# Multi-query attention: value scaling on GpSimd moved beside the VectorE exponential, a later first VectorE exponential, and a new plan

## The chip, the cores and the metric

The kernel runs on one core of one Trainium2 chip. The metric is device time in microseconds (us) of that core, from launch to the end of the program; lower is better. Before the change the median of three runs is 757.11 us (756.61 to 757.47). The profiled execution took 757.08 us, of which 755.2 us lie between its first and last instruction (the span), so a time is about 1.9 us more than its span.

## What is computed

The reference is attention with 16 query heads and one shared head of keys and values, for 8 batches, 1024 positions and a head dimension of 64, all in fp32:

```python
scores = q @ k.T / sqrt(64)
weights = exp(scores - max) / sum(exp(scores - max))
out = weights @ v
```

There are 8 x 16 x 1024 x 1024 = 134 million exponentials. The kernel does not subtract the maximum, and it gets the sum of the weights from a column of ones beside the values.

## The kernel before

Two heads are handled as a pair. There are 64 pairs (8 per batch), and each pair has 8 tiles of 128 keys. So there are 512 tiles, and each tile is scored in two halves of 512 queries: 1024 scores in all, each 128 keys by 2 heads by 512 queries. A score (`score`, L482) is two matmuls on TensorE that fill one of three PSUM buffers, `sc0` to `sc2`; I call them slots. A slot is free again when the exponential has read it.

The exponentials are split between two engines.

- Most are ACTIVATE instructions on ScalarE (ACT in the profile; `exp_act`, L496, recorded at L498), one per score, which write fp16 weights into a ring of 23 buffers `w`. Before the change there are 804 of them.
- The other 110 tiles (220 scores) are done by VectorE (DVE; `exp_dve`, L504). VectorE first reads each score from PSUM, scales it and writes a 16-bit integer, the `z` instruction (L512). When both halves are there, three or four more instructions on 128x2048 elements in SBUF build three terms `z`, `m` and `e` whose sum, with three scaled copies of the values, is the exponential's product: two masks (L529 and L532), a square of `m` (L524) and a product of `z` and `m` (L536). In the plan they are steps 0, 1, 2 and 3. Before the change step 2 squares only 1216 of the 2048 columns on VectorE, and GpSimd (POOL) squares the other 832 in two pieces of 416 (`sq`). Step 4 is the alternative: VectorE squares all 2048 columns. The plan takes it where more than `QUEUE` pieces are still waiting for GpSimd (L274).

The weights, which are laid out with keys on partitions, are the stationary operand of the value products (`value`, L555): 128x65 matmuls that accumulate into one of two PSUM buffers, for three groups of 6, 4 and 6 query blocks per pair (`BLOCKS`). A tile of ScalarE needs one value product per query block, a tile of VectorE three. In the plan an `av` is two such matmuls. After a group's last product VectorE takes the reciprocal of the sums (`rec`, L578) and multiplies (`norm`, L587), and the pair's output leaves by DMA.

Each batch needs its values three times, scaled by the three `TERMS` (`val`, L378). The first batch's are scaled on VectorE; the other seven batches' 21 scalings run on GpSimd. Both the pieces and these scalings are started by the helper `beside` of the kernel (L540): it adds a wait, so that the GpSimd instruction starts when the VectorE instruction before the chosen one has ended. So it runs beside the chosen one.

The order of the work on every engine is fixed when the program is built. `plan` (L56) walks through the work with a cost for each instruction, and the order in which it lets things happen is the order in which the instructions are recorded; on the chip an engine keeps that order and waits on semaphores. The planner's choices that matter here are these.

- Which tiles VectorE takes (L120 to L128): a tile is taken if the work waiting for VectorE is below `BACKLOG`, or `BACK_END` when at most `END` pairs are left, and none of the last `LAST` tiles is taken.
- When TensorE scores rather than multiplies values (L176 to L189, `MARGIN` and `WAIT`), and how far the value products lag behind the scores (L170, `LAG`, `RAMP`, `END_LAG`).
- `SPLIT`: for the last `SPLIT` tiles all first halves are scored before all second halves.
- What runs on GpSimd beside what: the planner's own `beside` (L71) takes the oldest waiting piece of work that has waited for an age. It is called for squares beside a `z` (L245), for values beside a `rec` (L256), and for both wherever they have waited longer than `PIECE_AGE` (L230).

At the start TensorE transposes keys and queries, VectorE copies them out of PSUM, and the second half of this is recorded between the first scores (`turn_first`, L442).

Of the kernel before, what the change touches and what calls it, by code (L numbers as in the profile page):

```python
# [20 lines left out]

ACT_P, ACT_L = 0.905, 1.19
QK_P, AV_B, AV_1, SWITCH, PE_L = 0.22, 0.0295, 0.02, 0.10, 0.49
MARGIN, WAIT = 0.318, 0.144
END, END_LAG = 5.567, -0.028
VEC = dict(z=1.13, rec=0.11, val=0.34)
NORM = 0.07, 0.067
STEPS = (0.6, 0.6, 0.7, 1.13)
WHOLE, QUEUE = 1.13, 3
PIECE, PIECE_T, PIECE_AGE = 416, 1.2, 11.627  # L30
VEC_L = 0.19
VEC_DEP = 0.12
BACKLOG, BACK_END = 8.576, 2.062
LAST, SPLIT, FIRST = 13, 7, 3
RAMP, VALS, COLD, WARM = 0.541, 3.0, 1, 0.0
BUSY = 20, 3, 5, 0
WBUFS = 23
ZBUFS = 6
LAG = 2.1
FAR = 1e9  # L40
BLOCKS = (0, 6, 10, 16)
STEP = 2
# [13 lines left out]
def plan(NP, NKT, HP=8):  # L56
# [6 lines left out]
    def vec(k, g):  # L63
        return NORM[0] + NORM[1] * size[g] if k == "norm" else VEC[k]
# [3 lines left out]
    def emit(t, *op):  # L68
        ops.append((t, len(ops), op))

    def beside(t, age, kinds):  # L71

        x = next((x for x in pool if x[0] <= t - age and x[1] in kinds), None)
        if x is None:
            return
        pool.remove(x)
        emit(t, *x[1:])
        if x[1] == "val":
            vdone[x[2:]] = t + PIECE_T
        elif x[3] == 1:  # L80
            squared.append((t + PIECE_T, x[2]))

    squared: list = []
    pe = act = dve = 0.0
    mode = ""
    slot = [0.0] * 3
    acc = [0.0] * 2
# [18 lines left out]
    while p < NP or groups:  # L106
        assert min(pe, dve) < 2e3
        if pe <= dve:
            T = pe
# [40 lines left out]
            for grp in groups:  # L150
# [7 lines left out]
                for j, k, x in left:  # L158
                    t = NKT * gp + j
# [9 lines left out]
            rest = (2 * NT - nq) / (2 * NKT)  # L169
            lag = min(LAG, END_LAG + (LAG - END_LAG) * rest / END, RAMP * nq / (2 * NKT))  # L170
            cost = AV_B * STEP * cold
# [18 lines left out]
            if do == "qk":  # L190
                s = min(free, key=lambda s: slot[s])
                st = max(T + (SWITCH if mode != "qk" else 0), slot[s])
                pe, mode = st + QK_P * cold, "qk"
# [6 lines left out]
                else:  # L200
                    u = units.pop(0)
                    act = max(act, st + PE_L + QK_P * (cold - 1))
# [5 lines left out]
            elif do == "av":  # L208
                st = max(T + (SWITCH if mode != "av" else 0), tav)
                pe, mode = st + cost + (AV_1 if mode == "qk" else 0), "av"  # L210
                grp, (j, k, x) = pick
                gp, gg, left, a, n, known = grp
                t = NKT * gp + j
# [11 lines left out]
            else:  # L225
                nxt = [x for x in slot + acc + [tav] if T < x < FAR] + [dve] * (dve > T)
                pe = max(min(nxt, default=0.0), T + 1e-3)
        else:
            T = dve
            beside(T, PIECE_AGE, ("sq", "val"))  # L230
            steps += [(x[1], len(STEPS) - 1) for x in squared if x[0] <= T]
            squared = [x for x in squared if x[0] > T]
# [6 lines left out]
            what, x = (free or todo or [("", None)])[0]  # L239
            if z:  # L240
                x = z[0]
                zs.remove(x)
                r, s, u = x
                T = max(T, r)
                beside(T, 0.3, ("sq",))  # L245
                emit(T, "z", *u)
                dve = T + VEC["z"]
                slot[s] = dve + VEC_L
                if u[1] == 1:
                    steps += [(u[0], n) for n in range(len(STEPS) - 1)]  # L250
                    ready[u[0], 1, "v"] = dve + VEC_L
                last = ("z", u[0])
            elif what == "ev":
                evs.remove(x)
                if x[1] == "rec":
                    beside(T, 0.3, ("val",))  # L256
                emit(T + late, *x[1:])
                dve = T + late + vec(x[1], x[3])
                if x[1] == "rec":
                    evs.insert(0, (T, "norm", *x[2:]))  # L260
                else:
                    acc[x[4]] = dve + VEC_L
                last = x
            elif what == "val":
                vals.remove(x)
                emit(T, "val", *x[1:])
                dve = T + VEC["val"]
                vdone[x[1:]] = dve + VEC_L
                last = None
            elif what == "step":  # L270
                steps.remove(x)
                dve = T + late + STEPS[x[1]]
                if x[1] == len(STEPS) - 2:
                    if sum(y[1] == "sq" for y in pool) > QUEUE:  # L274
                        x, dve = (x[0], len(STEPS)), T + late + WHOLE
                        steps.append((x[0], len(STEPS) - 1))
                    else:
                        pool += [(dve, "sq", x[0], n) for n in range(2)]
                emit(T + late, "step", *x)
                if x[1] in (0, len(STEPS) - 1):  # L280
                    ready[x[0], x[1] and len(TERMS) - 1, "v"] = dve + VEC_L
                last = x
            else:
                nxt = [x[0] for x in zs + evs + vals + squared if x[0] > T] + [pe + 1e-6] * (pe > T)
                dve = max(min(nxt, default=0.0), T + 1e-3)
                last = None
# [7 lines left out]
def kernel(  # L294
# [37 lines left out]

    wbuf = [consts.tile([P, 2, S], FP16, name=f"w{i}") for i in range(WBUFS)]
    order, vtiles = plan(NP, NKT, HP)

    writers: dict = {}
# [100 lines left out]
    def busy(n):  # L437

        for _ in range(n):
            nc.tensor.matmul(kst[0]["busy"][:, 0, 0:P], ident, ident, start=True, stop=True)  # L440

    def turn_first(n):  # L442
# [5 lines left out]
        if n == 0:  # L448
# [7 lines left out]
            for r in range(2):  # L456
                V(out=k16[:, 0:4, r, :], in_=kn[:, 0:4, :])
            busy(BUSY[0])
        parts = ((0, 2), (2, 4)) if n == 0 else ((4, NKT),)
# [6 lines left out]
        if n == 0:  # L466
            busy(BUSY[1])
        if n < 2:
# [7 lines left out]
        if n == 0:  # L476
            V(out=qn[0][:, 4:NKT, :], in_=qf[:, 4:NKT, :])
            for r in range(2):
                V(out=k16[:, 4:NKT, r, :], in_=kn[:, 4:NKT, :])
            busy(BUSY[2])  # L480

# [146 lines left out]
    with tc.manual_schedule(engines={ENG.PE, ENG.Activation, ENG.DVE, ENG.Pool}):  # L628
# [7 lines left out]
        for _, _, (op, *args) in order:  # L636
            if op == "qk":
# [7 lines left out]
                if scores < 3:  # L645
                    busy(BUSY[3])
                if scores == 3:
# [46 lines left out]
```

## Time and profile before

| | before |
|---|---|
| time, median of 3 runs | 757.11 us |
| span of the profiled execution | 755.2 us |
| TensorE matmul busy | 737.0 us (98%) |
| TensorE weight load busy | 493.1 us (65%) |
| VectorE busy | 710.3 us (94%) |
| ScalarE busy | 739.5 us (98%) |
| GpSimd busy | 335.3 us (44%) |
| ScalarE exponentials, first start and last end | 804, 6.57 us and 746.13 us |
| one `z` of VectorE (128x1024 from PSUM) | 1.21 us |
| one square of 1216 columns; product of 2048 columns | 0.78 us; 1.22 us |
| one piece of 416 columns on GpSimd | 0.87 us |
| one value scaling on GpSimd | 1.48 to 2.02 us |

Three engines look nearly full. To read which one sets the time, two things about the view are needed. An instruction's duration runs from its start to its end; on ScalarE an instruction can start before the one ahead of it has ended, so that durations overlap, and the pace is the distance between two starts or two ends, not the duration. And a matmul's end is modelled, so a busy TensorE need not be at its limit.

### The profile page before, as it was taken

What the parts mean: (1) busy time and instruction counts of PE and PEld (TensorE: products, weight loads), DVE (VectorE), ACT (ScalarE), POOL (GpSimd) and SP (SyncE); (2) the same over time, 40 slices, a digit from 0 to 9 for tenths busy, and PEclk for the clock granted to TensorE, in tenths of its full rate; (3) what the DMA queues carried; (4) which work ended last, traced back from release to release, by engine and by line L of the source; (5) the groups of instructions that cost most, each with busy time, mean ns of one, the idle gap of its engine ahead of it and who ended that gap; (6) DMA issues with size and microseconds to landing.
All of it is one profiled execution on the core that took longest, in us unless ns stands there. A gap on an engine that the chain in (4) does not pass through costs nothing.

```text
span 755.2 us, 30412 instructions
## 1 busy us (share of the span) xinstructions
PE 737.0 (98%) x13804; PEld 493.1 (65%) x13804; DVE 710.3 (94%) x1057; ACT 739.5 (98%) x806; POOL 335.3 (44%) x398
## 2 busy tenths in 40 slices
PE   7899999999999999999999999999999999999997
PEld 4455666666666666666666666666666666666676
DVE  6999999999999999999999999999999999999963
ACT  7999999999999999999999999999999999999995
POOL 2357434473444643446344564345533555343210
PEclk9999999999999999999999999999999999999999
DMA  6564555647556457675446756457644466644133
GB/s 129 89 99 103 89 103 89 107 89 111 114 107 107 95 86 105 121 111 102 92 74 122 135 88 101 76 98 134 121 87 88 77 127 115 104 78 100 34 86 86
DMA packets 179889, 75.10 MB, mean 99 GB/s; under 512 B 78384, under 2 KB 178736, under 8 KB 179760
## 3 DMA queue, kind: packets, MB, share of 16 engines
q1 hardware_dynamic: 140544, 54.01, 32.8%
q0 software_dynamic: 37744, 18.36, 21.5%
q8 instruction: 108, 1.77, 1.0%
q10 hardware_dynamic: 1472, 0.79, 0.4%
q14 instruction: 21, 0.17, 0.1%
HBM read 39.58 MB, written 33.55 MB: 97 GB/s over the span
## 4 chain that ended last, share of the span: by engine, by line
ACT 91%; PE 6%; DVE 2%; DMA 0%; issue 0%; DVEq 0%
ACT w_109 L498 4%; ACT w_112 L498 4%; ACT w_113 L498 4%; ACT w_111 L498 4%; ACT w_110 L498 4%; ACT w_114 L498 4%; ACT w_108 L498 4%; ACT w_102 L498 4%; ACT w_107 L498 4%; ACT w_98 L498 4%; ACT w_97 L498 4%; ACT w_106 L498 4%; ACT w_104 L498 4%; ACT w_96 L498 4%; ACT w_115 L498 4%; ACT w_100 L498 4%
## 5 line engine op out<-in xcount | busy, mean ns | idle before, releaser
L486 PEld LDWEIGHTS <-k2t_135 64*128 64x128 f16 x256 | 13.3, 94 | 20.2 <-issue 12.5
L486 PEld LDWEIGHTS <-k2t_1158 64*128 64x128 f16 x256 | 12.2, 93 | 10.7 <-issue 4.3
L486 PEld LDWEIGHTS <-k2t_14686 64*128 64x128 f16 x256 | 12.4, 93 | 9.2 <-issue 1.8
L486 PEld LDWEIGHTS <-k2t_7903 64*128 64x128 f16 x256 | 12.4, 93 | 8.2 <-issue 1.8
L486 PEld LDWEIGHTS <-k2t_5642 64*128 64x128 f16 x256 | 12.3, 93 | 8.2 <-issue 1.8
L486 PEld LDWEIGHTS <-k2t_12425 64*128 64x128 f16 x256 | 12.3, 93 | 8.2 <-issue 1.8
L486 PEld LDWEIGHTS <-k2t_10164 64*128 64x128 f16 x256 | 12.3, 93 | 8.2 <-issue 1.8
L486 PEld LDWEIGHTS <-k2t_3381 64*128 64x128 f16 x256 | 12.0, 93 | 7.8 <-issue 1.6
L565 PEld LDWEIGHTS <-w_100 128*128 128x128 f16 x288 | 12.9, 97 | 4.7 <-issue 4.7
L565 PEld LDWEIGHTS <-w_102 128*128 128x128 f16 x288 | 12.8, 97 | 4.5 <-issue 4.5
L565 PEld LDWEIGHTS <-w_104 128*128 128x128 f16 x288 | 12.9, 97 | 4.2 <-issue 4.2
L565 PEld LDWEIGHTS <-w_96 128*128 128x128 f16 x288 | 12.9, 98 | 4.1 <-issue 4.1
L565 PEld LDWEIGHTS <-w_106 128*128 128x128 f16 x288 | 13.0, 97 | 3.6 <-issue 3.6
L565 PEld LDWEIGHTS <-w_98 128*128 128x128 f16 x288 | 12.9, 97 | 3.7 <-issue 3.7
L565 PEld LDWEIGHTS <-w_115 128*128 128x128 f16 x272 | 12.2, 97 | 4.2 <-issue 4.2
L565 PEld LDWEIGHTS <-w_101 128*128 128x128 f16 x288 | 12.7, 97 | 3.3 <-issue 3.3
L565 PEld LDWEIGHTS <-w_105 128*128 128x128 f16 x288 | 12.7, 97 | 3.3 <-issue 3.3
L565 PEld LDWEIGHTS <-w_103 128*128 128x128 f16 x288 | 12.6, 97 | 3.4 <-issue 3.4
L565 PEld LDWEIGHTS <-w_97 128*128 128x128 f16 x288 | 12.7, 97 | 2.9 <-issue 2.7
L565 PEld LDWEIGHTS <-w_108 128*128 128x128 f16 x272 | 12.2, 97 | 3.5 <-issue 3.5
L565 PEld LDWEIGHTS <-w_113 128*128 128x128 f16 x272 | 12.2, 97 | 3.6 <-issue 3.6
L565 PEld LDWEIGHTS <-w_117 128*128 128x128 f16 x272 | 12.0, 97 | 3.8 <-issue 3.8
(5615 smaller groups left out, 3712.2 us busy)
## 6 DMA issues: line engine op xcount, KB each, us to landing
qf<-in_q_dram ACTq DMA_DIRECT2D x2, 256.0 KB, 3.8
qn_185<-in_q_dram POOLq DMA_DIRECT2D x1, 512.0 KB, 6.4
qn_328<-in_q_dram POOLq DMA_DIRECT2D x4, 128.0 KB, 3.9
qn_504<-in_q_dram POOLq DMA_DIRECT2D x4, 128.0 KB, 3.5
out_dram<-osb_501 SPq DMA_DIRECT2D x1, 512.0 KB, 3.2
out_dram<-osb_821 SPq DMA_DIRECT2D x1, 512.0 KB, 5.3
qn_1011<-in_q_dram POOLq DMA_DIRECT2D x4, 128.0 KB, 3.2
out_dram<-osb_1149 SPq DMA_DIRECT2D x1, 512.0 KB, 3.2
```

The source lines that it names most:

```text
L486: nc.tensor.matmul(sc[t, c][:, h, :], kst[p // HP]["k2t"][64 * h : 64 * h + 64, key(p // HP, j, h), :], qt[p][64 * h : 64 * h + 64, 4 * c ...
L498: ins = nc.scalar.activation(out=w, in_=sc.pop((t, c)), func=EXP, scale=ascale).ins
L565: nc.tensor.matmul(acc[p, grp][:, o : o + D + 1], w[:, h, i * P : (i + 1) * P], kst[p // HP]["v"][k][:, j, 0 : D + 1], start=(n == 0 and y ...
```

## The change

The diff does four things.

1. Values are scaled on GpSimd beside a `z` (which reads PSUM) and no longer beside a reciprocal. A scaling must have waited three times as long as a square before it is taken.
2. The planner's VectorE is taken to be ready only at 2.0 (`READY`), so that three scores go to ScalarE before the first one goes to VectorE; before, the first VectorE score was the second of all.
3. `QUEUE` falls from 3 to 1, so that step 4 (the whole square on VectorE) is chosen at times.
4. The planner's other constants get new values, and with all of this the order on every engine is a new one.

Counted from the order in which the two programs record their work:

| | before | after |
|---|---|---|
| ScalarE exponentials | 804 | 808 |
| tiles on VectorE (`z` instructions) | 110 (220) | 108 (216) |
| squares in pieces: VectorE parts, GpSimd pieces | 110, 220 | 82, 164 |
| whole squares on VectorE (step 4) | 0 | 26 |
| `av` (two value matmuls each) | 5856 | 5824 |
| runs of scores between value products | 650 | 616 |
| `av` after the last score | 112 | 115 |

```diff
-MARGIN, WAIT = 0.318, 0.144
-END, END_LAG = 5.567, -0.028
+MARGIN, WAIT = 0.284, 0.166
+END, END_LAG = 1.121, -0.195
...
-WHOLE, QUEUE = 1.13, 3
-PIECE, PIECE_T, PIECE_AGE = 416, 1.2, 11.627
+WHOLE, QUEUE = 1.13, 1
+PIECE, PIECE_T, PIECE_AGE = 416, 1.2, 10.459
...
-BACKLOG, BACK_END = 8.576, 2.062
-LAST, SPLIT, FIRST = 13, 7, 3
-RAMP, VALS, COLD, WARM = 0.541, 3.0, 1, 0.0
-BUSY = 20, 3, 5, 0
+BACKLOG, BACK_END = 7.719, 2.337
+LAST, SPLIT, FIRST = 12, 2, 3
+RAMP, VALS, COLD, WARM = 0.162, 3.0, 1, 0.0
+BUSY, READY = (20, 3, 5, 0), 2.0
...
-LAG = 2.1
+LAG = 1.753
...
-        x = next((x for x in pool if x[0] <= t - age and x[1] in kinds), None)
+        x = next(
+            (x for x in pool if x[0] <= t - age * (1 + 2 * (x[1] == "val"))
+             and x[1] in kinds), None)
...
-    pe = act = dve = 0.0
+    pe, act, dve = 0.0, 0.0, READY
...
-                beside(T, 0.3, ("sq",))
+                beside(T, 0.3, ("sq", "val"))
...
-                if x[1] == "rec":
-                    beside(T, 0.3, ("val",))
```

## The prediction

> **What bounds the kernel now.** I read the page first: its busy line and the chain that ended last.
>
> ```profile
> PE 737.0 (98%) x13804; PEld 493.1 (65%) x13804; DVE 710.3 (94%) x1057; ACT 739.5 (98%) x806; POOL 335.3 (44%) x398
> ...
> ACT 91%; PE 6%; DVE 2%; DMA 0%; issue 0%; DVEq 0%
> ```
>
> Three engines are above 90%, so busy shares alone do not decide. The chain says ScalarE (91%). To be sure, I read its pace in the timeline, start and duration of its last exponentials:
>
> ```profile
> 723.70 1.35 ACT L498 ACTIVATE w_118<-sc_0_17375 128x1024 f16<-128x1024 f32 x1
> 724.62 1.35 ACT L498 ACTIVATE w_118<-sc_1_17379 128x1024 f16<-128x1024 f32 x1
> ...
> 743.67 1.55 ACT L498 ACTIVATE w_105<-sc_1_17927 128x1024 f16<-128x1024 f32 x1
> 744.57 1.56 ACT L498 ACTIVATE w_106<-sc_1_17930 128x1024 f16<-128x1024 f32 x1
> ```
>
> The starts are 20.87 us apart over 23 exponentials, 0.907 each, but the durations grow, so starts run ahead of the work. The ends (start plus duration) go from 725.05 to 746.13: 0.9166 each. The ends give the true pace. The first three exponentials of the run show the same: starts 6.57, 7.49, 8.40 with durations 1.02, 1.02, 1.03 end at 7.59, 8.51, 9.43. Over the run the first ends at 6.57 + 1.02 = 7.60 and the last at 746.13: 738.5 us for 803 intervals. At 0.9167 they are 736.1. So ScalarE lost only 2.4 us between its first and last exponential. The waits name where:
>
> ```profile
> ACT w_108 L498 <- PE sc_0_1407 L486: 0.9, 1, 0.9
> ACT w_96 L498 <- PE sc_1_212 L486: 0.4, 1, 0.4
> ACT w_99 L498 <- PE sc_1_282 L486: 0.3, 1, 0.3
> ACT w_109 L498 <- PE sc_0_531 L486: 0.2, 1, 0.2
> ```
>
> Taken between ends rather than from idle time, the losses are 0.48 at 9.4 us (w_96), 0.40 at 13.6 (w_99), 0.29 at 31.4 (w_109), 0.24 at 70.2 (w_107), 1.01 at 72.3 (w_108) and 0.05 at 19.5: 2.46 in all. After 72.3 us no interval between ends is longer than 0.92. ScalarE is the bound without a gap for 674 us, and nothing that only makes TensorE or VectorE shorter can be seen in the time there.
>
> What caused these waits is in TensorE's waits, and in the timeline around 70 us:
>
> ```profile
> PE sc_1_212 L486 <- DVE z_206 L512: 1.3, 1, 1.3
> PE sc_0_1351 L486 <- DVE z_1317 L512: 0.8, 1, 0.8
> PE acc_0_1265 L565 <- DVE m_886 L536: 0.6, 1, 0.6
> PE sc_0_237 L486 <- DVE z_206 L512: 0.5, 1, 0.5
> ```
>
> ```profile
> 67.39 1.35 DVE L524 TENSOR_TENSOR m_1205<-m_1205 128x1216 f16<-128x1216 f16 x1
> ...
> 68.07 2.02 POOL L378 TENSOR_SCALAR vals_1_88<-vn_907 128x512 f16<-128x512 f32 x1
> ...
> 70.26 1.76 DVE L536 TENSOR_TENSOR m_886<-z_834,m_886 128x2048 f16<-128x2048 f16 x1
> ...
> 72.11 1.49 POOL L378 TENSOR_SCALAR vals_2_89<-vn_907 128x512 f16<-128x512 f32 x1 [1.18 <-DVE m_886 L536]
> ```
>
> The two early losses come from the very first VectorE exponential, z_206: VectorE is still copying queries, so z_206 holds a slot from the second score on until 9.31. The pair at 70.2 and 72.3 is the first batch of GpSimd scalings: a square of 1216 columns took 1.35 (0.78 elsewhere), a product 1.76 (1.22 elsewhere), beside GpSimd work; the late `z` and the late `m_886` stop TensorE.
>
> **What the Trainium skill says.** "Perfetto Trace Analysis", section "Identifying the Most-Contended Engine": for ScalarE and VectorE occupancy is a fair measure, for matmuls it is not, and weight-load share should be used. That fits: TensorE's 98% stands beside 65% weight load, and ScalarE's 98% is the one to believe. "SBUF — State Buffer", section "Who interferes with whom": a VectorE instruction with at most one SBUF input outside the two-port modes does not contend with GpSimd; one with two SBUF inputs contends with GpSimd's reads. "VectorE: DVE Perf Modes", section "Why PSUM operands drop a tier": with a PSUM operand the two-port mode is out. So a `z` is a good neighbour. The trace agrees: vals_2_89, beside a reciprocal and a `z` only, took 1.49; vals_1_88, which began beside a square, took 2.02, and that square 1.35. "TensorE: Matmul & The Clock Gate", section "What's actually happening": a quiet TensorE drops to half clock in windows of 3413 ns. The trace shows 0.50 granted at 28 to 31 us, after value products had nearly stopped from 22 to 26 us (0.2 us busy); the loss at 31.4 lies in it.
>
> **The change, part by part.**
>
> *Four more ScalarE exponentials* (804 to 808, counted from the order): 4 x 0.917 = +3.67 us. They lie on the bound; nothing hides them.
>
> *First VectorE exponential behind three scores.* Now scores 1 to 3 go to ScalarE, score 4 is the `z`, in the slot that the first exponential leaves at about 7.6; VectorE reaches it at about 8.2, as now (the copy ahead of it, 0.42 from 7.76, is unchanged), and gives it back at about 9.4. The fourth ScalarE score uses the slot freed at 8.5 (second exponential's end) and is there by 9.0 (0.39 for the matmuls), while ScalarE needs it at 9.4. The next one takes z's slot at 9.4 and is needed at 10.3. So both early losses go: -0.48 - 0.40 = -0.88. The first exponential still starts at 6.57: nothing ahead of it changes.
>
> *Values beside `z`.* 21 GpSimd scalings move; their time falls from 1.5 to 2.0 each to about 1.5, off the path. On the path are only the losses at 70 us, 1.25. Bounds: none or all of it goes. The order around it is new and the collision was with squares too, so I take three quarters: -0.94. The scaling now waits for the VectorE instruction ahead of a `z`; queued behind it on GpSimd are pieces of squares, for which products (L536) wait, and the DMA issues for queries. With 44% of GpSimd in use, less after, there is room for that. In later batches the same scalings cost ScalarE nothing (no long interval after 72.3).
>
> *VectorE.* Two tiles fewer: 2 x (2 x 1.21 + 0.68 + 0.68 + 0.78 + 1.22) = -11.6. 26 whole squares at 1.22 (the nearest row is the product of 2048 columns) for 0.78: +11.4. Net nothing: still some 710 busy, 94%, and 26 products that no longer wait for pieces, with GpSimd relieved of 56 x 0.87 = 49 us. TensorE has 64 value matmuls fewer, at 0.030 (six start 0.18 apart in the tail) -1.9. Both are hidden behind ScalarE.
>
> *Half clock at 31 us.* The new order leaves TensorE as quiet as the old one: 13 `av` between the 20th and the 34th score now, 10 in the new order. I keep the 0.29, so the difference is 0.
>
> *End.* The last score still takes a slot that was freed three exponentials before the last, and then TensorE has 115 `av` instead of 112 without idle time: 6 x 0.030 = +0.18. The output after it is the same.
>
> *New waits.* An irregular order could bring some: bounds 0 and 1.5 (as the whole of the losses at 70 us and a bit more). VectorE's slack is what guards against it; I take +0.2.
>
> Sum: 757.11 + 3.67 + 0.18 - 0.88 - 0.94 + 0.2 = 759.34, so 759.3 us.
>
> **Rivals.**
>
> *All losses go, none come:* 757.11 + 3.67 + 0.18 - 2.46 = 758.5, within 0.2% of before (up to 758.62). For it: the losses are few and the change aims at four of six. Against: the clock loss has no reason to go. This is the floor if ScalarE's pace stands. Chance 0.13.
>
> *VectorE becomes late:* whole squares put 26 x 0.44 us back in bursts; a late `z` holds a slot and stops TensorE, as z_1317 did for 0.8. With 2 us of such waits: 759.3 + 2 = 761.3. For it: VectorE is 97% busy between 150 and 550 us. Against: it is so now, and loses nothing. Chance 0.15.
>
> *The other side, faster:* ScalarE's pace would be TensorE's in truth, with scores just in time and 0.9035 between starts as ScalarE's own. Then time follows TensorE: -1.9 and -1.8 for the early losses, 753.4. For it: 44% of the exponentials start within 0.05 us of their score's modelled end. Against: ends spaced 0.917 even where starts are 0.903 apart, at the beginning and at the end. Chance 0.04.
>
> **Numbers.** My forecast has 0.68, and all of it is slower by over 0.2%. Slower 0.68 + 0.15 = 0.83; same 0.13; faster 0.04. The range goes from 758.0 (the floor 758.5, less the 0.5 by which single runs differ from the median) to 761.4 (the late VectorE).
>
> **What would show it.** Right: 808 exponentials ending 0.917 apart with under 2 us lost in all; no loss at 9.4 and 13.6; GpSimd scalings at 1.5; about 9.1 us from the last exponential's end to the end of the span, plus 0.2. Wrong: ends closer than 0.915, or long intervals after 100 us, or a first exponential that does not start at 6.57.

## The result, and the profile after

The changed kernel takes 761.39 us, the median of four runs (760.57 to 764.25), beside 757.26 for the kernel before on the same chip. By the medians it is slower by 4.1 us. The ratio, taken over all runs, is 1.0063 (95% interval 1.0036 to 1.009), which is 4.8 us. The forecast was 2.2. The profiled execution took 760.57, with a span of 758.8. First its page, busy line and chain that ended last:

```profile
PE 730.6 (96%) x13740; PEld 487.8 (64%) x13740; DVE 712.4 (94%) x1045; ACT 743.9 (98%) x810; POOL 286.4 (38%) x342
...
ACT 79%; PE 11%; DVE 6%; POOL 2%; issue 1%; POOLq 0%
```

GpSimd's busy time fell by the forecast 49 us, VectorE's is the same within 2, TensorE's is 6 lower, and ScalarE has four exponentials more. The busy shares explain nothing beyond those four. The chain does tell something: ScalarE has fallen from 91% to 79% of it, and GpSimd, which was not in it, has 2%. This points to waits of ScalarE behind work that ends on GpSimd, though chain shares alone don't show it. ScalarE's own waits (in all, times, longest) name the place:

```profile
ACT w_96 L498 <- PE sc_1_3910 L486: 1.3, 1, 1.3
...
ACT w_104 L498 <- PE sc_0_1184 L486: 0.2, 1, 0.2
ACT w_115 L498 <- PE sc_1_14985 L486: 0.2, 1, 0.2
```

I use one measure throughout: the ends of exponentials are 0.9167 apart, and what an interval between two ends is longer than that is a loss. A loss is placed at the end that comes late, but for those of 9.4 and 13.6 us, which keep the prediction's names (it placed them at the end before). With the losses, the span divides almost without a rest. The second column of measurements is a second profile of the same changed kernel (`e0_after_again` below); all are differences from the profile before, in us.

| term | predicted | after, span 758.8 | after again, span 760.3 |
|---|---|---|---|
| four more exponentials | +3.67 | +3.67 | +3.67 |
| start of the first one (6.57 before; 6.03, 6.37) | 0 | -0.55 | -0.20 |
| losses up to 80 us (2.47 before; 0.43, 1.55) | -1.82 | -2.04 | -0.92 |
| losses after 80 us (0 before; 2.69, 2.70) | +0.20 | +2.69 | +2.70 |
| last end to end of span (9.08 before; 8.90, 8.88) | +0.18 | -0.18 | -0.20 |
| sum | +2.23 | +3.59 | +5.05 |
| measured span less 755.2 | | +3.6 | +5.1 |

One term stands out: the losses after 80 us, the same in both executions, and thirteen times the 0.2 that I took for "new waits". The largest is 1.46 at 178 us, at w_96. I followed it back. TensorE's waits say that its score waited for a slot that a `z` held:

```profile
PE sc_1_3910 L486 <- DVE z_3743 L512: 1.9, 1, 1.9
```

The timeline of VectorE there (start, duration, line, operation, output and inputs; in brackets the idle time before it and what ended it):

```profile
168.60 1.22 DVE L512 TENSOR_SCALAR z_3743<-sc_0_3731 128x1024 uint16<-128x1024 f32 x1
...
169.83 1.06 DVE L532 TENSOR_SCALAR m_3695<-z_3607 128x2048 uint16<-128x2048 uint16 x1
...
171.14 2.06 DVE L524 TENSOR_TENSOR m_3695<-m_3695 128x1216 f16<-128x1216 f16 x1
173.96 1.23 DVE L536 TENSOR_TENSOR m_3278<-z_3173,m_3278 128x2048 f16<-128x2048 f16 x1 [0.77 <-POOL m_3278 L524]
...
175.80 1.21 DVE L512 TENSOR_SCALAR z_3743<-sc_1_3868 128x1024 uint16<-128x1024 f32 x1
```

And that of GpSimd:

```profile
166.56 1.49 POOL L378 TENSOR_SCALAR vals_1_85<-vn_3070 128x512 f16<-128x512 f32 x1 [1.93 <-DVE osb_3681 L587]
168.00 0.78 POOL L403 DMA_DIRECT2D qn_3692<-in_q_dram  x1
168.86 1.48 POOL L378 TENSOR_SCALAR vals_2_86<-vn_3070 128x512 f16<-128x512 f32 x1
170.30 0.75 POOL L403 DMA_DIRECT2D qn_3692<-in_q_dram  x1
171.07 0.89 POOL L524 TENSOR_TENSOR m_3278<-m_3278 128x416 f16<-128x416 f16 x1
171.90 0.76 POOL L403 DMA_DIRECT2D qn_3692<-in_q_dram  x1
172.68 1.24 POOL L524 TENSOR_TENSOR m_3278<-m_3278 128x416 f16<-128x416 f16 x1
```

Read together: both scalings take their 1.48 us beside a `z`, as intended. But the places beside a `z` are where the squares' pieces went before. The two pieces of tile 98 (m_3278) lose their places, grow older than `PIECE_AGE`, and the planner then starts them beside whatever VectorE does next. On the chip they start later still: GpSimd works almost without a pause from 166.56 until 174.64, on two scalings, two pieces and four DMA issues of 0.75 to 0.78 (`beside` in the kernel records a waiting issue behind each piece of work). So the first piece, recorded beside a reciprocal, starts 1.3 us after it and runs beside another tile's square of 1216 columns, which takes 2.06 instead of 0.78; the second, beside the same square, takes 1.24 instead of 0.87. The product of m_3278 must then wait 0.77 for GpSimd, and behind it in VectorE's order, after a reciprocal and a multiplication, stands the second half of z_3743, which starts at 175.80 although its score has been there since 173.6. Its slot stops TensorE for 1.9, and ScalarE for 1.3. The Trainium skill says in "SBUF — State Buffer", section "Who interferes with whom", that VectorE with two SBUF inputs contends with GpSimd's reads. The trace agrees: the square overlaps the two pieces by 0.82 and 0.52, together 1.34, and grew by 1.28.

Counted from the two orders, the pieces up to 700 us that do not run beside a `z` are 2 before (one of tile 28 at 67 us, one of tile 87 at 153) and 11 after, from tiles 35, 98, 183, 290, 327, 355 and 415. The losses at 178, 297, 504, 547 to 554 and 636 us follow such pieces within some 14 us. Those at 64 and 622 us (0.29 and 0.11) follow none, and behind the late pieces of tiles 35 and 290 (77 and 446 us) nothing is lost.

Three predicted details hold. No loss is left at 9.4 and 13.6, and the scalings take 1.48 to 1.50, all 21. The pace at the end is the old one; the last exponentials of the changed kernel end at 747.15, 748.06, 748.98 and 749.90:

```profile
745.63 1.52 ACT L498 ACTIVATE w_107<-sc_0_17738 128x1024 f16<-128x1024 f32 x1
746.55 1.51 ACT L498 ACTIVATE w_108<-sc_0_17743 128x1024 f16<-128x1024 f32 x1
747.45 1.53 ACT L498 ACTIVATE w_107<-sc_1_17786 128x1024 f16<-128x1024 f32 x1
748.36 1.54 ACT L498 ACTIVATE w_108<-sc_1_17789 128x1024 f16<-128x1024 f32 x1
```

### The profile page after: what moved, and what is told of

It reads as the page before. It is cut to its first block, busy times and chain, and to the rows that moved or that the text cites. A ratio compares the mean times of both kernels' runs of the same rounds, so it can differ in the third digit from the quotient of the medians.

```text
span 758.8 us, 30190 instructions
## 1 busy us (share of the span) xinstructions
PE 730.6 (96%) x13740; PEld 487.8 (64%) x13740; DVE 712.4 (94%) x1045; ACT 743.9 (98%) x810; POOL 286.4 (38%) x342
## 4 chain that ended last, share of the span: by engine, by line
ACT 79%; PE 11%; DVE 6%; POOL 2%; issue 1%; POOLq 0%
ACT w_97 L498 4%; ACT w_101 L498 4%; ACT w_98 L498 4%; ACT w_99 L498 4%; ACT w_100 L498 4%; ACT w_96 L498 4%; ACT w_102 L498 4%; ACT w_103 L498 4%; ACT w_104 L498 3%; ACT w_116 L498 3%; ACT w_108 L498 3%; ACT w_106 L498 3%; ACT w_118 L498 3%; ACT w_107 L498 3%; ACT w_117 L498 3%; ACT w_115 L498 3%
```

## The experiments

My theory: ScalarE's count sets the time, and the 2 us that I had not forecast are late pieces of squares, which the scalings have pushed from their places. Rivals: the whole squares come in bursts that make VectorE late; the half clock of TensorE near 30 us costs more in the new order (`RAMP`); or the scaling's place is irrelevant and the constants alone did it. The ratios are taken over all runs of both kernels, so they differ a little from the quotient of the two medians. Names of buffers carry no numbers in these traces, and lines move by the inserted ones.

### Are the late pieces the cause?

`e0_after_again` is the changed kernel unaltered, so that it shares its runs of before with the others.

> The changed kernel once more, beside the three that follow, with the profile of another execution. Theory (ScalarE is the bound; time is its 808 exponentials at 0.917 us plus the time that it loses waiting for scores): 760.5 to 762, 808 ends 0.917 apart, losses of 2 to 4 us that lie near 176, 296, 503, 547 and 621 to 635 us as before, since they belong to the order of the work. Rival (the losses are chance, of the clock or of DMA): losses of that size at other places.

761.98 us, ratio 1.0058 (1.0045 to 1.0071). The late losses lie at the same instructions with the same sizes (1.46, 0.16, 0.10, ...); the early ones differ, 1.55 instead of 0.43. So in this kernel the late losses belong to the order, and the early ones vary between executions.

`e1_whole_late` gives the squares of the seven tiles with late pieces back to VectorE (14 pieces, not the 13 of the expectation; 11 of them are late), in the same order:

```diff
+    order = whole(order, (35, 98, 183, 290, 327, 355, 415))
...
+        if op[0] == "sq" and op[1] in tiles:
+            continue
+        if op[0] == "step" and op[1] in tiles and op[2] == 2:
+            op = ("step", op[1], 4)
```

> The changed kernel in its own order, but the seven tiles of which a GpSimd piece ran beside something other than a z (35, 98, 183, 290, 327, 355, 415) are squared whole on VectorE; 13 pieces fewer on GpSimd, 7 x 0.44 = 3.1 us more on VectorE. Theory (pieces that missed their z collide with VectorE instructions in SBUF, VectorE gets late, a slot is held): the losses near 176, 296, 503, 547 and 621 to 635 us go, 1.5 to 2.5 us faster than the changed kernel. Rival (VectorE has too much to do, whole squares make it late): slower than the changed kernel by up to 3 us, losses in the same places or more of them.

759.68 us, ratio 1.0032 (1.0023 to 1.0041): 2.3 less than `e0_after_again` on the same chip. Losses after 80 us fell from 2.70 to 0.54, a single one at 621 us. VectorE at the place of before:

```profile
171.38 0.78 DVE L536 TENSOR_TENSOR m<-m 128x1216 f16<-128x1216 f16 x1
172.08 1.22 DVE L548 TENSOR_TENSOR m<-z,m 128x2048 f16<-128x2048 f16 x1
...
174.13 1.23 DVE L524 TENSOR_SCALAR z<-sc 128x1024 uint16<-128x1024 f32 x1
```

The square takes 0.78 again, the product waits for nothing, the `z` starts about 1.7 us earlier. This also rules out the bursts as the cause of these losses: seven more whole squares made the kernel faster. It is shown that the late pieces cost 2.2 to 2.3 us. How much of that comes from their place and how much from a GpSimd that is busy with DMA issues ahead of them isn't separated: no run took the issues away. What makes the 0.54 at 621 stays open.

`e6_valz` is the kernel before with part one of the change alone (values beside a `z`):

```diff
-                beside(T, 0.3, ("sq",))
+                beside(T, 0.3, ("sq", "val"))
...
-                if x[1] == "rec":
-                    beside(T, 0.3, ("val",))
```

> The kernel before with part one alone: values beside a z, with three times the age, and the old constants (QUEUE 3); the planner's order gives 810 ScalarE exponentials, and 20 squares' pieces before 700 us that run beside something other than a z (2 in the kernel before, 11 in the changed one). Theory (scalings take the places beside z from pieces; these age, run beside instructions in SBUF and make VectorE late): 6 x 0.917 = 5.5 us for the count and more lost after 80 us than the 2.2 us of the changed kernel, 3 to 6 us; 764 to 768. Rival (the late losses come from the new constants, not from the moved values): losses as before, 762.4 or less.

772.34 us, ratio 1.0205 (1.019 to 1.0219), far slower than either theory expected. It has 810 ScalarE exponentials, 6 more than before (5.5 us), and 20 late pieces up to 700 us. ScalarE's waits of `e6_valz`, and below them those of `e1_whole_late`:

```profile
ACT w L498 <- PE sc L486: 14.6, 19, 1.4
```

```profile
ACT w L510 <- PE sc L498: 1.8, 3, 1.1
```

Late losses are 13.9 in the profiled execution, which at 775.60 us was the slowest of five. They can't all be put down to the 20 pieces: 6.1 of them lie between 270 and 289 us, where no piece counts as late. GpSimd of `e6_valz` there:

```profile
262.40 0.88 POOL L524 TENSOR_TENSOR m<-m 128x416 f16<-128x416 f16 x1 [8.21 <-PE sc L486]
263.22 0.78 POOL L403 DMA_DIRECT2D qn<-in_q_dram  x1
264.08 1.48 POOL L378 TENSOR_SCALAR vals<-vn 128x512 f16<-128x512 f32 x1
265.52 0.75 POOL L403 DMA_DIRECT2D qn<-in_q_dram  x1
266.30 0.89 POOL L524 TENSOR_TENSOR m<-m 128x416 f16<-128x416 f16 x1
267.12 0.76 POOL L403 DMA_DIRECT2D qn<-in_q_dram  x1
267.90 1.33 POOL L524 TENSOR_TENSOR m<-m 128x416 f16<-128x416 f16 x1
```

The order gives two pieces of work to each of two `z` that start at 262.14 and 264.15, and with the DMA issues between them the last piece starts 3.75 us after its `z`. A product at 267.22 waits 1.84 for a piece, TensorE is busy for only 5.5 of the 9 us up to 271, and from 270.4 to 277.2 it is granted half clock. So this run shows that part one with the old constants makes matters much worse, and that GpSimd can be late without a piece that counts as late; it gives no price for one piece. The new constants give back most of it; `QUEUE` (whole squares when more than one piece waits) may be the one that does, but no run changed it alone.

`e8_const_ready` is the reverse, the changed kernel without part one: constants and `READY` alone.

```diff
-                beside(T, 0.3, ("sq", "val"))
+                beside(T, 0.3, ("sq",))
...
+                if x[1] == "rec":
+                    beside(T, 0.3, ("val",))
```

> The changed kernel without part one: values beside a reciprocal as before, new constants, first z behind three scores; 810 ScalarE exponentials and one piece before 700 us beside something other than a z. Theory: 5.5 us for the count, 0.9 back at the start, under 1 us lost after 80 us; 760.5 to 762.5, losses of up to 1.3 near 70 us where the first scalings stand. Rival (new constants make the late losses): more than 2 us lost after 80 us, 763 or more.

763.23 us, ratio 1.0087 (1.0071 to 1.0104), with 810 exponentials. I had expected less than 1 us lost after 80 us; it was 2.65, with one late piece, and nothing is lost near that one. The profiled execution was again the slowest of five (765.38), and 1.10 of the 2.65 lies at 583 to 586 us, in and behind a window of half clock (580.1 to 583.5). My expectation missed that a scaling beside a reciprocal can itself do harm. GpSimd and then VectorE of `e8_const_ready`, ahead of its loss of 0.59 at 255 us:

```profile
246.45 1.95 POOL L378 TENSOR_SCALAR vals<-vn 128x512 f16<-128x512 f32 x1
...
249.15 0.89 POOL L524 TENSOR_TENSOR m<-m 128x416 f16<-128x416 f16 x1
...
251.49 2.36 POOL L378 TENSOR_SCALAR vals<-vn 128x512 f16<-128x512 f32 x1
```

```profile
248.56 2.04 DVE L529 TENSOR_SCALAR e<-z 128x2048 uint16<-128x2048 uint16 x1
...
251.27 1.23 DVE L524 TENSOR_TENSOR m<-m 128x2048 f16<-128x2048 f16 x1
252.41 1.22 DVE L512 TENSOR_SCALAR z<-sc 128x1024 uint16<-128x1024 f32 x1
```

A reciprocal of 0.2 us cannot cover 1.5 us of GpSimd. The scalings meet squares and take 1.95 and 2.36; the piece behind the first one and a DMA issue comes after its `z` (246.96 to 248.18) and meets a mask, which takes 2.04 instead of 0.68. The `z` at 252.41 is then late and TensorE waits 0.98 for it.

`e14_late_rec` measures that place by itself: `e1_whole_late` with each scaling moved to the next reciprocal and nothing else moved (but for the DMA issue that `beside` may record behind it). It ran beside `e1_again`, a repeat of `e1_whole_late`.

```diff
+        if op[0] == "val" and op[1] > 0:
+            held.append(x)
+            continue
+        if op[0] == "rec" and held:
+            out.append(held.pop(0))
```

> The changed kernel with its seven late tiles squared whole, and in this same order the 21 scalings moved from their z to the next reciprocal; 808 exponentials, VectorE, ScalarE and TensorE in the same order. Theory (a scaling beside a reciprocal reaches into masks and squares and stretches them): scalings at 1.9 to 2.4 us, masks of 1 us and more beside them, 0.5 to 3 us lost after 80 us, slower than e1 by as much. Rival (the place of a scaling does not matter where no piece is late): within 0.5 us of e1, nothing more lost.

> The changed kernel with its seven late tiles squared whole, once more, as the neighbour of e14 on the same chip: 759.0 to 760.2, with 0.5 us lost near 619 us and little else after 80 us.

762.04 us (760.97 to 762.53) for `e14_late_rec`, 759.76 (759.1 to 760.2) for `e1_again`: the place beside a reciprocal costs 2.3 us. The scalings (min, median, max in ns, first and last start) of `e14_late_rec`, then of `e1_again`:

```profile
L404 POOL TENSOR_SCALAR vals<-vn x21: 1479/1934/2582, 74.6 to 634.9; 128x512 f16<-128x512 f32 x21
```

```profile
L390 POOL TENSOR_SCALAR vals<-vn x21: 1482/1488/2000, 68.9 to 625.7; 128x512 f16<-128x512 f32 x21
```

Losses after 80 us are 2.93 against 0.55, and neither profile has half clock between 80 and 750 us. So part one does what it is for, and in this order it is worth about 2.3 us. The pieces that it pushes aside take about 2.3 back.

### Is ScalarE's count the bound?

`e3_fewer_products` is the kernel before without the second-term products of VectorE's tiles (but for a group's first and last), for less TensorE work.

```diff
+        if k == 1 and n > 0 and not end:
+            return
```

> The kernel before, with the products of the second term left out for VectorE's tiles (but for a group's first and last), which takes about 850 pairs of value matmuls or some 50 us of work from TensorE and nothing from ScalarE; its output is not the reference's. Theory (ScalarE is the bound): within 1 us of before, 755.5 to 757.5. Rival (TensorE is the bound and ScalarE waits for just-in-time scores; ScalarE's own pace is 0.9035): 10 us or more faster, 747 or less, and ends under 0.91 apart.

756.71 us, ratio 0.9996 (0.9986 to 1.0007). Its page:

```profile
PE 709.6 (94%) x12046; PEld 452.1 (60%) x12046; DVE 710.0 (94%) x1057; ACT 739.6 (98%) x806; POOL 335.1 (44%) x398
```

There are 1758 matmuls fewer, 53 us at 0.030, and 27 us less TensorE busy time; the time is the same and the ends stay 0.917 apart. TensorE is not the bound, which ends the rival on the other side. (That rival counted 44% of exponentials as starting within 0.05 us of their score's end; in the trace of before it is 47 to 48%, and still no sign of a bound.)

`e4_end802` takes two exponentials off ScalarE by the change's end constants alone:

```diff
-END, END_LAG = 5.567, -0.028
+END, END_LAG = 1.121, -0.195
```

> The kernel before with END and END_LAG at their new values and nothing else: the planner gives VectorE one more tile near the end, so 802 ScalarE exponentials and not 804. Theory (ScalarE's count sets the time): 2 x 0.917 = 1.8 us faster than before, some 755.0. Rival (VectorE is as full as ScalarE): no gain, or slower by up to 2 us with losses after 650 us.

759.82 us, ratio 1.0043 (1.0029 to 1.0057); I had expected 755.0. The last exponential did end earlier (745.09, not 746.13), but this order leaves 180 `av` after the last score, not 112: 68 x 2 x 0.030 = 4.1 us. From the last exponential to the end it takes 13.4 instead of 9.1. The losses, 3.4 in the profiled execution, are 0.9 more than before. So this run doesn't price the count: for that the tail must be held still.

`e11_best` and `e12_after_fixed` hold it still: the orders of before and after, both freed of late pieces and with the same head and the same extra matmuls (see below). They differ in the count, 804 and 808, and in the rest of the order.

> The kernel before with the three repairs together: its first eight scores in the changed kernel's order, the warming matmuls, tiles 28 and 87 squared whole. Theory (804 exponentials at 0.917 us and almost nothing lost): 754.3 to 755.2, 2 to 2.5 us faster than before and all losses together under 0.5 us. Rival (losses only move): 756 or more.

> The changed kernel with its seven late tiles squared whole and the warming matmuls; 808 exponentials. Theory (with the losses gone only the count is left): 757.1 + 3.7 - 2.4 = 758.4, 757.8 to 759.0, some 3.7 us more than the repaired kernel before. Rival (the new order has something of its own beyond the count and the losses): 759.5 or more though nothing is lost between the ends, or a faster pace, 757 or less.

758.17 and 761.71 us (ratios 1.0013 and 1.0058), so 3.54 between them. Both are some 3 us above what I had expected, for the extra matmuls cost more than they save (`e9_warm` below). From the profiles: 4 x 0.9167 = 3.67, losses 3.74 and 3.48 (-0.26), tail and start +0.28: 3.69, and the spans differ by 3.7. The count term fits to 0.1 us.

### The head and the half clock

`e5_head` is the kernel before with the changed kernel's first eight scores (three to ScalarE, the fourth to VectorE).

```diff
+    order = head(order)
```

> The kernel before in its own order, but for its first eight scores, which take the order that they have in the changed kernel (three scores for ScalarE ahead of the first z); 804 exponentials. Theory: the two losses at 9.4 and 13.6 us go, 0.9 us faster than before (0.8 to 1.0), everything later alike. Rival (the wait only moves to the next slot or into a later start of the value products): within 0.3 us of before, with a new loss before 25 us.

757.07 us, ratio 0.9996 (0.9988 to 1.0005). The loss at 9.4 is gone and 0.38 at 13.6 stays. In the profiled execution a longer window of half clock cost 0.89 between 28 and 35 us (0.29 before), and the first exponential started 0.22 later. That is where the gain went in this execution; over 13 runs none shows either.

`e2_ramp` gives the changed kernel the old `RAMP`, so that value products start earlier.

```diff
-RAMP, VALS, COLD, WARM = 0.162, 3.0, 1, 0.0
+RAMP, VALS, COLD, WARM = 0.541, 3.0, 1, 0.0
```

> The changed kernel with RAMP at its old value 0.541 (value products follow the scores later at the start), again 808 ScalarE exponentials. Theory of the half clock (what the changed kernel loses beyond its profile, in runs with a mean clock of 0.987 to 0.993, comes from half-clock windows of TensorE in the first 100 us): clock back to 0.997, runs within 1 us of each other, about 0.5 to 1 us faster than the changed kernel. Rival (the order later on decides): same spread as the changed kernel, time within 1 us of it either way.

764.54 us, ratio 1.0102 (1.0084 to 1.0119). The old value doesn't help: the early losses grew (2.63 up to 80 us), and late ones came, 5.2 in all. But the profiled execution, 767.37, was the slowest of five, and it had more half clock and not less (10.2 us from 24.8, 6.8 from 48.7, 3.4 from 642.6; 2.8 of the late losses stand at that last one). Any constant changes the whole order, so this doesn't test the half clock.

`e9_warm` leaves the order as before and adds four 128x128 matmuls ahead of each of scores 13 to 40, to keep TensorE from going quiet.

```diff
+        for _ in range(4 if 12 <= len(scored) < 40 else 0):
+            nc.tensor.matmul(sc[t, c][:, 0, 0:P], ident, ident, start=True, stop=True)
```

> The kernel before with four more 128x128 matmuls ahead of each of the scores 13 to 40 (identity by identity, into the slot that the score then overwrites), 0.22 us of TensorE each time in a stretch where it has few value products. Theory (TensorE's quiet stretch near 20 to 30 us brings half-clock windows, and these cost ScalarE the losses of 28 to 34 us, 0.3 in the profile of before and up to 1.3 in others): no half clock before 60 us, nothing lost between 20 and 50 us, 0.3 to 1 us faster than before with less spread. Rival (the losses there are of the order, not of the clock): clock back to full but the losses stay, or scores 0.2 us later and a slower kernel.

759.64 us, ratio 1.0034 (1.0021 to 1.0046). No half clock was seen, but the scores came late instead: losses between 12 and 40 us grew to 3.9 (before it was 0.74). Dearer than what it cures.

How much the half clock itself varies is seen in the profile after, and below it in that of `e0_after_again` (stretch, length, busy us of PE, PEld, DVE, ACT, POOL with counts, granted clock, DMA share, GB/s):

```profile
28.00:32.00 4.00, 3.36 (x59) 2.00 (x55) 4.00 (x8) 4.00 (x6) 1.79 (x3) 1.00 0.53 83
```

```profile
28.00:32.00 4.00, 3.89 (x44) 2.23 (x44) 3.45 (x7) 3.93 (x5) 1.32 (x3) 0.50 0.53 72
```

The same program, one time at full clock and one time at half. In these two executions it loses 0.14 and 1.26 us between 20 and 50 us. And there is something else in both: a second window of half clock near 60 us, with a loss of 0.29 behind it, where the kernel before ran at full clock. Before, after and `e0_after_again`:

```profile
60.00:66.00 6.00, 5.76 (x111) 3.84 (x108) 6.00 (x8) 6.00 (x8) 4.70 (x5) 1.00 0.51 62
```

```profile
60.00:64.00 4.00, 3.97 (x50) 2.23 (x49) 3.76 (x8) 3.81 (x5) 2.40 (x3) 0.65 0.74 93
```

```profile
60.00:64.00 4.00, 3.75 (x33) 1.86 (x33) 3.77 (x7) 4.00 (x5) 3.53 (x4) 0.61 0.71 102
```

The mean granted clock says the same over more runs: 0.990 to 0.996 in the six of `e0_after_again`, 0.993 in the mean, against 0.997 in the mean of the 25 runs of before beside them.

### What made the losses near 70 us, and the best version

`e10_whole28` is the kernel before with the squares of tiles 28 and 87, the only ones with late pieces, done whole.

> The kernel before in its own order, but tiles 28 and 87, the two before 700 us with a piece beside something other than a z, are squared whole on VectorE; values stay beside reciprocals. Theory (the late piece of tile 28, not the scalings' place, made the losses at 70.2 and 72.3 us): these 1.25 us go, 755.5 to 756.2. Rival (the scaling beside a reciprocal made them, as the prediction had it): losses at 70 to 72 us of 1 us or more stay, time within 0.4 us of before.

755.95 us, ratio 0.9983 (0.9976 to 0.999). The losses of 0.24 and 1.01 at 70 to 74 us are gone, here and in `e13_head28` below, though a scaling there, still beside a reciprocal, takes 2.08. It was the late piece, not the scaling's place, that had made them. (The profiled execution, 757.42 us, lost 2.0 in its head and 0.69 at 545 us, more than the median suggests; neither lies at the edited tiles.)

`e13_head28` puts the two cures of the kernel before together:

```diff
+    order = head(order)
+    order = whole(order, (28, 87))
```

> The kernel before with its first eight scores in the changed kernel's order and tiles 28 and 87 squared whole, without warming matmuls; 804 exponentials. Theory (what the head saves is lost again at 28 to 34 us under a half clock): as tile 28's repair alone, 755.5 to 756.4, nothing lost after 50 us. Rival (the head's gain adds up): 754.5 to 755.2.

755.66 us (755.02 to 756.12), ratio 0.9983 (0.9975 to 0.9991): faster than both kernels, if by 0.9 us only, and no faster against before than `e10_whole28` without the new head. So the head's gain is not shown here either. Its page:

```profile
PE 735.9 (98%) x13804; PEld 494.0 (66%) x13804; DVE 709.8 (94%) x1057; ACT 739.1 (98%) x806; POOL 330.9 (44%) x394
...
ACT 94%; PE 5%; DMA 0%; DVE 0%; issue 0%
```

ScalarE's share of the chain is 94%, the highest of all, and one loss of 0.38 is left in 803 intervals; this execution had no half clock inside the run. At the 0.917 between ends, only fewer exponentials on ScalarE, or a shorter head or tail, could still help such an execution.

## Why the prediction was right in direction and short in size

- **What bounds the kernel.** Right. ScalarE's ends, 0.917 apart, and its count decide (`e3_fewer_products`, and 3.54 us between `e11_best` and `e12_after_fixed`, where 3.67 was forecast). Reading ends rather than starts was what kept the forecast on the slower side.
- **First `z` behind three scores, -0.88.** Both losses are gone in the changed kernel, as forecast. That the new head alone does it is not shown: in `e5_head` the 0.38 at 13.6 stayed, and the time did not move. The first exponential started at 6.03 and 6.37 instead of 6.57; over the executions and kernels here it varies from 6.03 to 6.86, so 0 was fair.
- **Values beside `z`, -0.94.** The loss near 70 us did go, by 1.25, but I had given the scaling as its cause, and `e10_whole28` shows that a late piece was. I had the fact before me, a square of 1.35 us beside GpSimd, and asked only about one of the two GpSimd instructions near it.
- **New waits, +0.2: the step that failed.** Its words were "VectorE's slack is what guards against it", and of GpSimd "With 44% of GpSimd in use, less after, there is room for that." The pieces and the DMA issues queued behind the scalings were named, and then dismissed by an average share. The share did fall, to 38%, and counted from the two orders 6 of 220 `z` had no GpSimd work beside them before and 44 of 216 after. Yet pieces were late, since the scalings of a batch took three `z` within 6 us, and where that happened GpSimd was full: it had hardly a pause in the 8 us before 174.64, shortly ahead of the largest loss. The late losses are 2.7 us; 2.2 to 2.3 of them are the late pieces (`e1_whole_late`). My upper bound of 1.5 was too low as well. It was sized from the losses at 70 us, which are what one late piece cost there; the order recorded 11 of them, and I hadn't counted them.
- **VectorE work nets to nothing.** Right (712.4 and 710.3 us). "26 products that no longer wait for pieces" was true too, but the pieces that were left waited more.
- **Half clock, difference 0.** A second, smaller miss. I compared TensorE's work only around the 20th to 34th score. The changed kernel has another window near 60 us; in and behind its windows it lost 0.43 and 1.55 in two executions, against 0.29 in one of before. So the difference was 0.1 and 1.3, and how it spreads over more executions is not measured.
- **End, +0.18.** Measured -0.18 and -0.20; too small to matter.
- **The rival "VectorE becomes late", 761.3.** It gave nearly the measured time, and a late `z` holding a slot is what stopped TensorE. But its cause, whole squares in bursts, is refuted for these losses: whole squares are the cure. That my range reached up to 761.4, as far as the measured median, is owed to this rival, and so was luck.

With 2.7 in place of 0.2 and -0.2 in place of +0.18, the sum is 761.5. The other differences, the whole loss at 70 us, the start and the half clock, take it to 760.7 for the first profiled execution (760.57) and to 762.2 for the second (762.03).

## What to carry to other kernels

Where work of a second engine is placed beside chosen instructions of a first one, the resource is the places, their spacing and the second engine's time around them, not the mean busy share: count, from the recorded order, how many pieces end up outside their places and how many share one, and add what else stands in that engine's queue, here DMA issues. One such piece in the trace before shows what it can cost, not what each will: here the late pieces of one tile cost from nothing to 1.6 us. When an item is moved to a better place, ask what stood in that place and where it goes now. And a constant of a planner changes the whole order; to price one item, edit the finished order.

## What was not expected of the hardware

- The granted clock in the first 70 us differs between executions of one program: the changed kernel had half clock at 21.9 to 25.3 us in one and at 26.8 to 33.6 in another; between 20 and 50 us that went with losses of 0.14 and 1.26 us. Single runs of the kernel before range from 756.02 to 759.45 us on one chip, so a difference of 1 us between single runs says nothing.
- When VectorE and GpSimd instructions meet, both can grow, and VectorE's up to threefold: a square from 0.78 to 2.06, a mask from 0.68 to 2.04; on GpSimd a scaling from 1.48 to 2.58, a piece from 0.87 to 1.93 (at 628 us of the changed kernel).
- A scaling beside a `z` costs neither of them anything: 1.22 for the `z` at 168.60 in the changed kernel, 1.48 for the scaling; all 216 `z` of that profile took 1.18 to 1.23. But the scaling outlasts the `z`, and the mask that follows pays: the one at 169.83 overlaps the scaling by 0.51 and takes 1.06 instead of 0.68.
